# One pool of weight halves for the whole kernel, and one set of four small tiles

## The chip, the core and the metric

The kernel runs on one core of a Trainium2 chip. The metric is the device time of one execution in microseconds (us); the time before is the median of three runs, 2027.32 us. TensorE (PE) multiplies, VectorE (DVE) and ScalarE (ACT) do elementwise work, GpSimd (POOL) does a little elementwise work and issues some DMAs, and SyncE (SP) issues most DMAs.

## What is computed

The reference is a decoder trunk of two layers over one sequence of 256 tokens with width 2048, all in float32. The even layer projects its normed input into two latents (q and kv, 512 wide each), a rotary key of 64 and a pooling input of 1024, runs attention with 8 heads and a pooling mixer, and projects out. The odd layer is a gated short convolution. Each layer ends with a squared-ReLU MLP with hidden width 8192:

```
def _mlp(h, w_up, w_down):
    return jnp.square(jax.nn.relu(h @ w_up)) @ w_down

x = x + jnp.concatenate([a, b], axis=-1) @ even_w_out[e]        # even layer
x = x + _short_conv(h, odd_w_in[o], odd_conv_w[o], odd_w_out[o])  # odd layer
x = x + _mlp(_rmsnorm(x, mlp_norm_g[layer]), w_mlp_up[layer], w_mlp_down[layer])
```

The pooling mixer takes, in four groups of 256 channels, trailing means over 2, 4, 8 and 16 positions minus the token, then a small linear map per group.

## The kernel before

Float32 products are made from two halves: every weight and every activation is split into a part `hi` that the fast float32r format holds and a rest `lo`, and a product is three matmuls (hi by hi, lo by hi, hi by lo).

Weights come in slabs of about 1 MB. `slab` (L123) takes a tile `raw` from a pool of three and issues its DMA on SP (L128). `halved` (L131) then makes for each part of the slab one tile `hi` by a cast on ACT (L140) and one tile `lo` by a subtraction on DVE (L141). The pool `halves` has six buffers of each; a slab takes two of each, so three slabs can be held ready ahead of PE. A `raw` tile is free again when its subtractions are done, a `hi` or `lo` tile when its last matmul is done.

The pools `raws` and `halves` are opened by `new_stage` (L77). It is called with three raw buffers twice: at L213 for the first stage and at L393 after it. The second call closes both pools and opens them anew over the same memory with `reuse_waits="tile"`, which means that a new tile waits for the old tiles that it overlaps. The first stage (`latent_slab`, L334) reads eight slabs of 2 x 1088 columns for the latents and the rotary key, so its `hi` and `lo` rows have 4.25 KB; all later slabs have rows of 4 KB. The tiles of the second opening lie at other addresses than those of the first, and one new tile overlaps two old ones. After L393 the eight slabs of the pooling input follow (loop over the four groups, L463 on), then four slabs of the kv weights and three of the q weights (`widen`, L513), one slab of the pooling map, the output projection with attention woven in, and the MLPs and the convolution. The calls at L714 and L900 keep `raws` and `halves` and only change what lies above them.

Between the last latent matmul and the first pooling matmul stand, on PE, a transpose of gain rows (L238) and, on ACT, six copies out of PSUM (`lat`, L366). The rotary tables are made on DVE from L395 on.

Small tiles come from the pool `small` with two buffers for each name. Name `t` holds the copied half of a PSUM sum (`sum_halves`, L191), the discarded squares (`junk`, L288, L385, L505) and the rotated part (`turned`, L497). Name `u` holds the sum itself, the pooled mean (`pm`, L487) and the sums of forms (`f`, L743). Name `sq` holds the squared hidden values (L731) and the gated values (L943), and `rb` (L315) a spread-out norm factor. All of them have rows of up to 2 KB.

Each engine works through its own queue in order. The order within a queue is not the order of the source: a planner of the framework sets it when the kernel is built, from its own estimate of when each instruction can start, with the source order as priority. `with behind(...)` (L114) adds fixed order at some places. An instruction at the head of a queue that waits for a semaphore stops all behind it. The pooled mean of the last group is split only behind the preparation of the first q slab (L567 to L569).

Of the kernel before, what the change touches and what calls it, by code (L numbers as in the profile page):

```python
# [16 lines left out]
P = 128  # L17
D = 2048
S = 256
# [48 lines left out]
def trunk(ctx: ExitStack, tc, x_in, pos_in, mix_g, mlp_g, w_up, w_down, w_in, pool_in, qa_g, kva_g, w_uq, w_ukv,  # L68
# [8 lines left out]
    def new_stage(raw_bufs=0, **more):  # L77

        for s_ in reversed(stage[1 - bool(raw_bufs):]):
            s_.close()  # L80
        del stage[1 - bool(raw_bufs):]
        for wanted in (dict(raws=raw_bufs, halves=6) if raw_bufs else {}, more):
            if wanted:
                stage.append(ExitStack())
                for name, bufs in wanted.items():
                    pools[name] = stage[-1].enter_context(tc.tile_pool(name=uid(name), bufs=bufs, reuse_waits="tile"))

    pools = {}
    small = ctx.enter_context(tc.tile_pool(name="small", bufs=2))
    acts = ctx.enter_context(tc.tile_pool(name="acts", bufs=4))  # L90
    psum = ctx.enter_context(tc.tile_pool(name="psum", bufs=4, space=PSUM))

# [2 lines left out]
    def uid(s):  # L95
        count[0] += 1
        return f"{s}{count[0]}"
# [4 lines left out]
    def act_tile():  # L102
        return acts.tile([P, 4, 2 * S], F32R, tag="hT", name=uid("hT"))
# [86 lines left out]

    def sum_halves(ps, name):  # L191

        t = small.tile([P, 2, S], F32, tag="t", name=uid("t"))
        nc.scalar.copy(t, ps[:, :, S:2 * S])  # L194
        u = small.tile([P, 2, S], F32, tag="u", name=uid(name))
        nc.vector.tensor_tensor(out=u, in0=ps[:, :, 0:S], in1=t, op=ALU.add)
        return u

    def split(dst_hi, dst_lo, src):
        nc.scalar.copy(dst_hi, src)  # L200
        nc.vector.tensor_tensor(out=dst_lo, in0=src, in1=dst_hi.bitcast(F32), op=ALU.subtract)
# [83 lines left out]
    def squares(ss, b):  # L285

        for t in range(T):
            junk = small.tile([P, NB], F32, tag="t", name=uid("junk"))  # L288
            nc.scalar.activation(junk, x[:, t, b * NB:(b + 1) * NB], AF.Square, accum_out=ss[:, t, b:b + 1])

    def turn_block(xT, b, which, i, then=None):
# [19 lines left out]
    def over_tokens(r, pool):  # L311

        ps = bank2()
        for t in range(T):
            rb = small.tile([P, P], F32, tag="rb", name=uid("rb"))  # L315
            nc.vector.tensor_copy(rb, r[:, t:t + 1].to_broadcast([P, P]))
            nc.tensor.transpose(ps[:, 0, t * P:(t + 1) * P], rb, ident)
        R = pool.tile([P, S], F32, name=uid("R"), bufs=1)
        nc.vector.tensor_copy(R, ps[:, 0, 0:S])
        return R  # L320
# [49 lines left out]
    def latents():  # L370

        lat_ss = ap_.tile([P, 2 * T], F32, name="lat_ss")
        for i, g in ((1, "kva"), (0, "qa")):
            dst = act_tile()
            ps = bank2().rearrange("p a (k s) -> p (a k) s", s=S)
            for k in range(KL):
                c0 = i * LORA + k * P
                for t in range(T):
                    nc.tensor.transpose(ps[:, k, t * P:(t + 1) * P], lat[:, t, c0:c0 + P], ident)
            for k in range(KL):  # L380
                split_scaled(dst[:, k, 0:S], dst[:, k, S:2 * S], ps[:, k, :], gain(g, k))
            latT.append(dst)
        for t in range(T):
            for i in range(2):
                junk = small.tile([P, NB], F32, tag="t", name=uid("junk"))  # L385
                nc.scalar.activation(junk, lat[:, t, i * LORA:(i + 1) * LORA], AF.Square,
                                     accum_out=lat_ss[:, i * T + t:i * T + t + 1])
        rsqrt(lat_r, lat_ss, LORA)
        R0.append(over_tokens(r0, ap_))
# [73 lines left out]
    for g in reversed(range(GROUPS)):  # L463
        ps = bank2()
        for s in range(2):
            ws = slab(pool_in[g, s], 8, 2 * P, sub=4)
            for j in range(8):
                kt = 8 * s + j
                for n in range(2):
                    columns_summed(ps[:, n, 0:S], xT, kt, ws[j], n * P, kt == 0, kt == KD - 1)  # L470
            if s == 0:
                flush()
        if done:
            split_pooled(*done)
        u = ap_.tile([P, 2, PAD + S], F32, tag="s", name=uid("pu"), bufs=4)
        nc.gpsimd.memset(u[:, :, 0:PAD], 0.0)
        nc.vector.tensor_tensor(out=u[:, :, PAD:], in0=ps[:, :, 0:S], in1=twice(R0[0]), op=ALU.mult)
        cur = u
        for st in range(g + 1):
            sh = 1 << st  # L480
            nxt = ap_.tile([P, 2, PAD + S], F32, tag="s", name=uid("pn"), bufs=4)
            if st < g:
                nc.gpsimd.memset(nxt[:, :, 0:PAD], 0.0)
            nc.gpsimd.tensor_tensor(out=nxt[:, :, PAD:], in0=cur[:, :, PAD:], in1=cur[:, :, PAD - sh:PAD + S - sh],  # L484
                                    op=ALU.add)
            cur = nxt
        m = small.tile([P, 2, S], F32, tag="u", name=uid("pm"))  # L487
        nc.gpsimd.tensor_scalar(out=m, in0=cur[:, :, PAD:], scalar1=1.0 / (2 << g), scalar2=None, op0=ALU.mult)
        nc.gpsimd.tensor_tensor(out=m[:, :, 0:PAD], in0=cur[:, :, PAD:2 * PAD],
                                in1=invc[:, g, :].unsqueeze(1).to_broadcast([P, 2, PAD]), op=ALU.mult)  # L490
        nc.gpsimd.tensor_tensor(out=m, in0=m, in1=u[:, :, PAD:], op=ALU.subtract)
        done = g, m

    def rotate(src, t, heads, tables):

        own, other = (a[:, t, :].unsqueeze(1).to_broadcast([P, heads, ROPE]) for a in tables)
        turned = small.tile([P, heads, ROPE], F32, tag="t", name=uid("turned"))  # L497
        for a, b in ((slice(0, HALF), slice(HALF, ROPE)), (slice(HALF, ROPE), slice(0, HALF))):
            nc.vector.tensor_tensor(out=turned[:, :, a], in0=src[:, :, b], in1=other[:, :, a], op=ALU.mult)
        nc.vector.tensor_tensor(out=src, in0=src, in1=own, op=ALU.mult)  # L500
        nc.vector.tensor_tensor(out=src, in0=src, in1=turned, op=ALU.add)

    def square_sum(out_, a):
        n = a.shape[1]
        junk = small.tile([P, NB], F32, tag="t", name=uid("junk"))  # L505
        nc.scalar.activation(junk[:, :n], a, AF.Square, accum_out=out_)


# [201 lines left out]
    def mlp(layer, ss, xT, after=None):  # L710
# [6 lines left out]
        def up_chunk(c):  # L717

            pss = []
            yield from columns_steps(pss, up, xT, c * NB, 4)  # L720
            hT = act_tile()
            seven = c < 2 * (pairs - 1)
            if seven:
                fT = pools["forms"].tile([P, 2, 2, 4, P], F32R, tag="fT", name=uid("fT"))
            hid[c] = hT
            if seven:
                sums[c] = fT
            for i, ps in enumerate(pss):
                u = sum_halves(ps, "h")
                nc.scalar.activation(u, u, AF.Relu)  # L730
                sq = small.tile([P, 2, S], F32, tag="sq", name=uid("sq"))  # L731
                nc.scalar.activation(sq, u, AF.Square)
                split(hT[:, 2 * i:2 * i + 2, 0:S], hT[:, 2 * i:2 * i + 2, S:2 * S], sq)
                if seven:
                    sum_forms(fT[:, i], sq.rearrange("p e (t s) -> p (e t) s", t=T))
                yield
            if not r2:
                r2.append(const.tile([P, T], F32, name=uid("r2")))
                nc.vector.reciprocal(out=r2[0], in_=mean_eps(ss))

        def sum_forms(fT, a):

            f = small.tile([P, 4, P], F32, tag="u", name=uid("f"))  # L743
            nc.vector.tensor_tensor(out=f[:, 0:2, :], in0=a[:, 1:2, :].to_broadcast([P, 2, P]), in1=a[:, 0:4:3, :], op=ALU.subtract)
            nc.vector.tensor_tensor(out=f[:, 2, :], in0=a[:, 3, :], in1=f[:, 0, :], op=ALU.subtract)
            nc.vector.tensor_tensor(out=f[:, 3, :], in0=a[:, 2, :], in1=f[:, 2, :], op=ALU.subtract)
            split(fT[:, 0], fT[:, 1], f)
# [156 lines left out]
    for blk in range(4):  # L904
# [35 lines left out]
        yT.append(yt)  # L940
        for i in range(2):
            u = sum_halves(pss[i], "b")
            y = small.tile([P, 2, S], F32, tag="sq", name=uid("y"))  # L943
            nc.vector.tensor_tensor(out=y, in0=u, in1=accs[i], op=ALU.mult)
            split(yt[:, 2 * i:2 * i + 2, 0:S], yt[:, 2 * i:2 * i + 2, S:2 * S], y)

# [51 lines left out]
```

## Time and profile before

| | us |
|---|---|
| median of the three runs | 2027.32 |
| lowest, highest | 2025.16, 2027.45 |
| the profiled execution, its own time | 2022.49 |
| its span, first to last instruction | 2020.7 |
| PE busy in the span | 2004.3 |
| DVE busy | 1392.5 |
| ACT busy | 1122.9 |
| POOL busy | 101.2 |

Busy times are those of the profiled execution. PE is busy for 99% of the span, so a time is gained or lost only where PE waits or works at a lower clock; the place to look is where the few waits of PE stand and what ends them.

### The profile page before, as it was taken

Reading aid. Unit: us, or ns where it says so; the run is one execution under the profiler, and the core shown is the slowest. Engines: PE = TensorE matmul, PEld = TensorE weight load, DVE = VectorE, ACT = ScalarE, POOL = GpSimd, SP = SyncE. Lnnn points to the kernel's source line nnn. Section 1 sums busy time; section 2 is a strip of 40 time slices with the busy share of each in tenths; the row PEclk is TensorE's granted clock in tenths of the full one; section 3 lists DMA queues with packets and bytes.
Section 4 is the critical chain, followed back from the end, with each engine's and each line's share of the span. In section 5 each row is a group of like instructions: output and inputs, shape, how many; then the busy total and the mean of one; then the engine's idle time right before and its main releaser. Section 6 shows DMA issues by size and latency. Waiting matters only on the chain.

```text
span 2020.7 us, 26714 instructions
## 1 busy us (share of the span) xinstructions
PE 2004.3 (99%) x10534; PEld 1721.2 (85%) x10534; DVE 1392.5 (69%) x1739; ACT 1122.9 (56%) x1480; POOL 101.2 (5%) x132
## 2 busy tenths in 40 slices
PE   8999999999999999999999999999999999999999
PEld 7987888888888888888888888888888888888887
DVE  5767567777767777776566656567776777767774
ACT  5467556655555655555444444456555566555552
POOL 2240000000000000000000000000000000000000
PEclk9999999999999999999999999999999999999999
DMA  7445657887888878765555557658797977879663
GB/s 255 159 168 185 194 202 227 273 250 236 276 260 269 250 237 273 240 211 185 188 188 188 187 188 240 218 188 239 243 278 243 289 231 261 262 249 286 200 219 125
DMA packets 65230, 457.62 MB, mean 226 GB/s; under 512 B 7344, under 2 KB 8240, under 8 KB 10192
## 3 DMA queue, kind: packets, MB, share of 16 engines
q1 hardware_dynamic: 56656, 396.91, 54.7%
q0 software_dynamic: 8416, 59.00, 15.3%
q8 instruction: 82, 1.34, 0.3%
q14 instruction: 44, 0.36, 0.0%
q10 hardware_dynamic: 32, 0.01, 0.0%
HBM read 453.79 MB, written 2.10 MB: 226 GB/s over the span
## 4 chain that ended last, share of the span: by engine, by line
PE 96%; POOL 1%; DMA 1%; DVE 1%; ACT 1%; issue 1%; SPq 0%; ACTq 0%; DVEq 0%; POOLq 0%
PE ps L160 32%; PE ps L161 16%; PE ps L153 10%; PE ps L155 10%; PE ps L154 10%; PE ps L769 4%; PE ps L771 4%; PE ps L770 4%; PE ps L297 1%; DMA raw<-in_even_w_in 1%; POOL pn L484 1%; PE ps L166 1%; PE ps L168 1%; PE ps L167 0%; DVE lo L141 0%
## 5 line engine op out<-in xcount | busy, mean ns | idle before, releaser
L141 DVE TENSOR_TENSOR lo<-raw,hi 128x1024 fp32r<-128x1024 f32 (+2 forms) x694 | 848.0, 1225 | 420.8 <-ACT hi L140 419.2
L140 ACT CAST hi<-raw 128x1024 fp32r<-128x1024 f32 (+2 forms) x694 | 726.1, 1049 | 592.9 <-PE ps L160 340.5
L160 PE MATMUL ps<-xT,hi 128*128 128x512 f32 x2816 | 989.0, 394 | 0.0
L161 PE MATMUL ps<-xT,lo 128*128 128x256 f32 x2816 | 789.5, 280 | 0.0
L160 PEld LDWEIGHTS ps<-xT,hi 128*128 128x128 f32 x2816 | 529.6, 188 | 122.2
L161 PEld LDWEIGHTS ps<-xT,lo 128*128 128x128 f32 x2816 | 527.6, 187 | 3.7
L153 PE MATMUL ps<-hi,hT 128*128 128x512 f32 (+1 forms) x896 | 349.1, 390 | 0.0
L155 PE MATMUL ps<-hi,hT 128*128 128x512 f32 (+1 forms) x896 | 347.3, 388 | 0.0
L154 PE MATMUL ps<-lo,hT 128*128 128x512 f32 (+1 forms) x896 | 347.1, 387 | 0.0
L153 PEld LDWEIGHTS ps<-hi,hT 128*128 128x128 f32 x896 | 168.3, 188 | 35.1 <-issue 1.3
L155 PEld LDWEIGHTS ps<-hi,hT 128*128 128x128 f32 x896 | 168.2, 188 | 34.7
L154 PEld LDWEIGHTS ps<-lo,hT 128*128 128x128 f32 x896 | 168.3, 188 | 33.3
L140 ACT CAST hi<-t 128x1024 fp32r<-128x1024 f32 x84 | 88.1, 1053 | 91.7 <-PE ps L160 50.7
L141 DVE TENSOR_TENSOR lo<-t,hi 128x1024 fp32r<-128x1024 f32 x84 | 102.6, 1221 | 48.7 <-ACT hi L140 48.7
L763 POOL DMA_DIRECT2D t<-in_w_mlp_down x42 | 36.6, 871 | 1135.0 <-DVE lo L141 821.5
L769 PE MATMUL ps<-hi,fT 128*128 128x512 f32 x224 | 88.1, 393 | 0.0
L771 PE MATMUL ps<-hi,fT 128*128 128x512 f32 x224 | 87.7, 391 | 0.0
L770 PE MATMUL ps<-lo,fT 128*128 128x512 f32 x224 | 87.1, 389 | 0.0
L194 ACT COPY t<-ps 128x512 f32<-128x512 f32 x88 | 50.8, 578 | 50.9 <-PE ps L161 50.9
L769 PE MATMUL ps<-hi,hT 128*128 128x512 f32 x168 | 65.8, 392 | 0.0
L771 PE MATMUL ps<-hi,hT 128*128 128x512 f32 x168 | 65.6, 390 | 0.0
L770 PE MATMUL ps<-lo,hT 128*128 128x512 f32 x168 | 65.4, 389 | 0.0
(186 smaller groups left out, 1573.6 us busy)
## 6 DMA issues: line engine op xcount, KB each, us to landing
raw<-in_w_mlp_up SPq DMA_DIRECT2D x128, 1024.0 KB, 5.3
raw<-in_w_mlp_down SPq DMA_DIRECT2D x114, 1024.0 KB, 5.2
raw<-in_odd_w_in SPq DMA_DIRECT2D x48, 1024.0 KB, 4.9
t<-in_w_mlp_down POOLq DMA_DIRECT2D x42, 1024.0 KB, 9.6
raw<-in_even_w_out SPq DMA_DIRECT2D x16, 1024.0 KB, 5.0
raw<-in_odd_w_out SPq DMA_DIRECT2D x16, 1024.0 KB, 5.0
t<-in_w_mlp_down SPq DMA_DIRECT2D x14, 1024.0 KB, 4.8
v<-in_w_mlp_down SPq DMA_DIRECT2D x14, 1024.0 KB, 4.9
```

The costliest lines, as they stand in the source:

```text
L140: a = nc.scalar.copy(h, r)
L141: v = nc.vector.tensor_tensor(out=l, in0=r, in1=h.bitcast(F32), op=ALU.subtract)
L153: nc.tensor.matmul(o, lhsT=a_hi, rhs=hi[:, c0:c0 + n], start=first, stop=False)
L154: nc.tensor.matmul(o, lhsT=a_hi, rhs=lo[:, c0:c0 + n], start=False, stop=False)
L155: nc.tensor.matmul(o, lhsT=a_lo, rhs=hi[:, c0:c0 + n], start=False, stop=last)
L160: nc.tensor.matmul(o, lhsT=hi[:, c0:c0 + P], rhs=act[:, kt, :], start=first, stop=False)
L161: nc.tensor.matmul(o[:, S:2 * S], lhsT=lo[:, c0:c0 + P], rhs=act[:, kt, 0:S], start=False, stop=last)
L194: nc.scalar.copy(t, ps[:, :, S:2 * S])
L763: nc.gpsimd.dma_start(b, at(e, n), accum_op=ALU.add)
L769: nc.tensor.matmul(o, lhsT=a_hi, rhs=hi, start=q == 0, stop=False)
L770: nc.tensor.matmul(o, lhsT=a_hi, rhs=lo, start=False, stop=False)
L771: nc.tensor.matmul(o, lhsT=a_lo, rhs=hi, start=False, stop=q == 3)
```

## The change

The pool of halves is opened once, ahead of all other pools that change, and is no longer part of `new_stage`, which now opens and closes only the raw tiles. Its rows are 4.25 KB throughout. In `small`, the names `t`, `u`, `sq` and `rb` become one name `t` with four buffers of 2 KB; `f` has a name and one buffer of its own. `sum_halves` adds in place, relu squared is squared in place, and the tile of sums of forms is taken inside `sum_forms`.

```diff
-        for wanted in (dict(raws=raw_bufs, halves=6) if raw_bufs else {}, more):
+        for wanted in (dict(raws=raw_bufs) if raw_bufs else {}, more):
...
-    pools = {}
+    pools = dict(halves=ctx.enter_context(tc.tile_pool(name="halves", bufs=6)))
     small = ctx.enter_context(tc.tile_pool(name="small", bufs=2))
+    T4 = dict(tag="t", bufs=4)
...
-        t = small.tile([P, 2, S], F32, tag="t", name=uid("t"))
-        nc.scalar.copy(t, ps[:, :, S:2 * S])
-        u = small.tile([P, 2, S], F32, tag="u", name=uid(name))
-        nc.vector.tensor_tensor(out=u, in0=ps[:, :, 0:S], in1=t, op=ALU.add)
+        u = small.tile([P, 2, S], F32, name=uid(name), **T4)
+        nc.scalar.copy(u, ps[:, :, S:2 * S])
+        nc.vector.tensor_tensor(out=u, in0=ps[:, :, 0:S], in1=u, op=ALU.add)
...
-            junk = small.tile([P, NB], F32, tag="t", name=uid("junk"))
+            junk = small.tile([P, NB], F32, name=uid("junk"), **T4)
...
-            rb = small.tile([P, P], F32, tag="rb", name=uid("rb"))
+            rb = small.tile([P, P], F32, name=uid("rb"), **T4)
...
-        m = small.tile([P, 2, S], F32, tag="u", name=uid("pm"))
+        m = small.tile([P, 2, S], F32, name=uid("pm"), **T4)
...
-        turned = small.tile([P, heads, ROPE], F32, tag="t", name=uid("turned"))
+        turned = small.tile([P, heads, ROPE], F32, name=uid("turned"), **T4)
...
                 nc.scalar.activation(u, u, AF.Relu)
-                sq = small.tile([P, 2, S], F32, tag="sq", name=uid("sq"))
-                nc.scalar.activation(sq, u, AF.Square)
-                split(hT[:, 2 * i:2 * i + 2, 0:S], hT[:, 2 * i:2 * i + 2, S:2 * S], sq)
-                if seven:
-                    sum_forms(fT[:, i], sq.rearrange("p e (t s) -> p (e t) s", t=T))
+                nc.scalar.activation(u, u, AF.Square)
+                split(hT[:, 2 * i:2 * i + 2, 0:S], hT[:, 2 * i:2 * i + 2, S:2 * S], u)
+                sum_forms(c, i, u.rearrange("p e (t s) -> p (e t) s", t=T))
...
-            f = small.tile([P, 4, P], F32, tag="u", name=uid("f"))
+            f = small.tile([P, 4, P], F32, tag="f", name=uid("f"), bufs=1)
...
-            y = small.tile([P, 2, S], F32, tag="sq", name=uid("y"))
+            y = small.tile([P, 2, S], F32, name=uid("y"), **T4)
```

The other discarded squares change their name in the same way. No instruction is added or removed.

## Rows read from the trace of the kernel before

**Rows 1.** The page: busy time by engine, and the chain by engine.
```profile
PE 2004.3 (99%) x10534; PEld 1721.2 (85%) x10534; DVE 1392.5 (69%) x1739; ACT 1122.9 (56%) x1480; POOL 101.2 (5%) x132
...
PE 96%; POOL 1%; DMA 1%; DVE 1%; ACT 1%; issue 1%; SPq 0%; ACTq 0%; DVEq 0%; POOLq 0%
```

**Rows 2.** Stretches: us, busy and count by engine, PE clock, DMA share, GB/s.
```profile
60.00:66.00 6.00, 4.07 (x27) 3.80 (x25) 0.33 (x2) 3.89 (x8) 0.00 (x0) 1.00 0.00 0
67.40:70.80 3.40, 3.40 (x18) 3.40 (x18) 1.96 (x4) 3.40 (x10) 0.47 (x1) 0.50 0.45 106
70.80:74.20 3.40, 3.40 (x31) 3.40 (x30) 3.15 (x4) 3.40 (x6) 0.55 (x1) 1.00 0.50 207
75.00:115.00 40.00, 40.00 (x341) 40.00 (x340) 28.65 (x33) 16.05 (x23) 22.20 (x20) 1.00 0.54 192
115.00:155.00 40.00, 40.00 (x186) 33.42 (x185) 28.32 (x58) 29.85 (x80) 14.36 (x14) 1.00 0.52 187
160.00:2015.00 1855.00, 1855.00 (x9592) 1580.82 (x9591) 1287.69 (x1539) 1029.37 (x1285) 53.31 (x68) 1.00 0.72 229
```

**Rows 3.** Waits of PE: who, for whom, us in total, times, longest.
```profile
PE ps L166 <- ACT hi L140: 1.9, 1, 1.9
PE ps L166 <- ACT qkv L520: 1.9, 1, 1.9
```

**Rows 4.** Timeline of PE: start us, us, instruction [idle before, releaser].
```profile
63.77 0.26 PE L238 MATMUL ps<-ident,rows 112*128 112x112 f32 x1
65.97 0.39 PE L166 MATMUL ps<-xT,hi 128*128 128x256 f32 x1 [1.93 <-ACT hi L140]
```

**Rows 5.** Timeline of ACT, the same moment.
```profile
50.19 0.47 ACT L204 ACTIVATE xT<-ps,gains 128x256 fp32r<-128x256 f32 x1 [0.55 <-DVE xT L205]
62.11 2.87 ACT L366 ACTIVATE lat<-ps,r 128x384 f32<-128x384 f32 x6 [11.45 <-PE ps L155]
64.86 2.00 ACT L140 CAST hi<-raw 128x1024 fp32r<-128x1024 f32 x2
```

**Rows 6.** Timeline of SP's queue: the first DMA issues for the pooling input.
```profile
41.95 0.33 SPq L128 DMA_DIRECT2D raw<-in_pool_in  x1
47.70 0.80 SPq L128 DMA_DIRECT2D raw<-in_pool_in  x2
```

**Rows 7.** DMA issues: count, KB each, median us from issue to landing.
```profile
raw<-in_pool_in SPq DMA_DIRECT2D x8, 1024.0 KB, 4.9
```

**Rows 8.** Timeline of DVE: the spread norm factor, and around the boundary.
```profile
43.08 0.36 DVE L316 COPY rb<-r 128x128 f32<-128x128 f32 x2 [0.85 <-POOL r L362]
...
64.07 0.27 DVE L239 COPY gains<-ps 128x112 f32<-128x112 f32 x1 [5.35 <-PE ps L238]
65.94 2.36 DVE L141 TENSOR_TENSOR lo<-raw,hi 128x1024 fp32r<-128x1024 f32 x2 [1.60 <-ACT hi L140]
```

**Rows 9.** Groups by form to 200 us, ACT: count, busy us, mean ns, idle.
```profile
L140 ACT CAST hi<-raw 128x1024 fp32r<-128x1024 f32 x47 | 47.9, 1048 | 14.5 <-PE ps L155 6.1 <-DMA raw<-in_even_w_out 2.8 <-DMA raw<-in_even_w_uq 2.6
L140 ACT CAST hi<-raw 128x1088 fp32r<-128x1088 f32 x15 | 16.2, 1100 | 7.9 <-DMA raw<-in_even_w_in 5.1 <-PE ps L155 2.7
```

**Rows 10.** Groups over the span: two operations of the MLP on DVE.
```profile
L196 DVE TENSOR_TENSOR h<-ps,t 128x512 f32<-128x512 f32 x64 | 44.0, 687 | 16.7 <-ACT t L194 16.7
...
L744 DVE TENSOR_TENSOR f<-sq 128x256 f32<-128x256 f32 x56 | 23.6, 422 | 8.5 <-ACT sq L732 8.5
```

**Rows 11.** Timeline of ACT: casts ahead of the copies out of PSUM.
```profile
138.06 1.05 ACT L140 CAST hi<-raw 128x1024 fp32r<-128x1024 f32 x1 [2.49 <-DMA raw<-in_even_w_uq]
...
149.31 1.05 ACT L140 CAST hi<-raw 128x1024 fp32r<-128x1024 f32 x1 [2.79 <-DMA raw<-in_even_w_out]
...
155.88 1.25 ACT L520 ACTIVATE qkv<-ps,lat_r 128x512 f32<-128x512 f32 x2
```

**Rows 12.** Timeline of DVE: a rotation, and the last read of a pooled mean.
```profile
88.87 1.42 DVE L499 TENSOR_TENSOR turned<-lat,other 128x32 f32<-128x32 f32 x2
...
138.30 0.69 DVE L201 TENSOR_TENSOR hT<-pm,hT 128x512 fp32r<-128x512 f32 x1
```

More of the change, by code (lines that the diff above doesn't have):

```diff
@@ L384, in latents @@
             for i in range(2):
-                junk = small.tile([P, NB], F32, tag="t", name=uid("junk"))
+                junk = small.tile([P, NB], F32, name=uid("junk"), **T4)
                 nc.scalar.activation(junk, lat[:, t, i * LORA:(i + 1) * LORA], AF.Square,
@@ L504, in square_sum @@
         n = a.shape[1]
-        junk = small.tile([P, NB], F32, tag="t", name=uid("junk"))
+        junk = small.tile([P, NB], F32, name=uid("junk"), **T4)
         nc.scalar.activation(junk[:, :n], a, AF.Square, accum_out=out_)
@@ L720, in up_chunk @@
             yield from columns_steps(pss, up, xT, c * NB, 4)
-            hT = act_tile()
-            seven = c < 2 * (pairs - 1)
-            if seven:
[L724 to L727, printed above, removed]
+            hT = hid[c] = act_tile()
             for i, ps in enumerate(pss):
@@ L730, in up_chunk @@
                 nc.scalar.activation(u, u, AF.Relu)
-                sq = small.tile([P, 2, S], F32, tag="sq", name=uid("sq"))
-                nc.scalar.activation(sq, u, AF.Square)
-                split(hT[:, 2 * i:2 * i + 2, 0:S], hT[:, 2 * i:2 * i + 2, S:2 * S], sq)
-                if seven:
-                    sum_forms(fT[:, i], sq.rearrange("p e (t s) -> p (e t) s", t=T))
+                nc.scalar.activation(u, u, AF.Square)
+                split(hT[:, 2 * i:2 * i + 2, 0:S], hT[:, 2 * i:2 * i + 2, S:2 * S], u)
+                sum_forms(c, i, u.rearrange("p e (t s) -> p (e t) s", t=T))
                 yield
@@ L739, in up_chunk, with sum_forms @@
                 nc.vector.reciprocal(out=r2[0], in_=mean_eps(ss))
-        def sum_forms(fT, a):
-            f = small.tile([P, 4, P], F32, tag="u", name=uid("f"))
+        def sum_forms(c, i, a):
+            if c >= 2 * (pairs - 1):
+                return
+            if i == 0:
+                sums[c] = pools["forms"].tile([P, 2, 2, 4, P], F32R, tag="fT", name=uid("fT"))
+            fT = sums[c][:, i]
+            f = small.tile([P, 4, P], F32, tag="f", name=uid("f"), bufs=1)
             nc.vector.tensor_tensor(out=f[:, 0:2, :], in0=a[:, 1:2, :].to_broadcast([P, 2, P]), in1=a[:, 0:4:3, :], op=ALU.subtract)
```

## The prediction

> **What bounds the kernel now.** First the page: PE is busy 2004.3 us of 2020.7, 99%, and 96% of the chain that ended last is PE's own matmuls [rows 1]. So the busy times of DVE and ACT do not matter as such; only a moment in which PE stands still, or works at the lower clock, can be won or lost. Next the table by stretches: from 160 us to the end PE is busy 1855.00 of 1855.00 us at clock 1.00 [rows 2]. There run both MLPs, with all 64 squared-ReLU sums and all 56 sums of forms that the diff rewrites [rows 10], and no wait there reaches PE. From 75 to 155 us PE is busy throughout too. What is left is the first 160 us, and there the waits of PE name two places after the start: one wait of 1.9 us for ACT's cast `hi`, and one of 1.9 us for ACT's copy `qkv` out of PSUM [rows 3].
>
> The first stands at the stage boundary of L393, which the diff touches. PE ends the latent matmuls and transposes the gain rows at 63.77; the first pooling matmul comes at 65.97, after 1.93 us of waiting [rows 4]. ACT's timeline shows why: it ran nothing from 50.7 us on, then waited 11.45 us at the head of its queue for PE, made the six copies `lat` from 62.11, and only then, at 64.86, the first two casts of a pooling slab [rows 5]. The slab itself was long there: its DMA was issued at 41.95, the next two at 47.70 [rows 6], and such a DMA lands 4.9 us after its issue [rows 7], so the first was in by about 46.9. DVE had sat idle 5.35 us before 64.07 and began the subtractions at 65.94 [rows 8]. Data and both engines were free, hence what kept the casts behind 62.11 was either room for `hi` and `lo` or the planned order. In the code the room is the plain candidate: the second pool lies over the first at other addresses, and its first tiles overlap tiles that the last two latent slabs still fill.
>
> [...]
>
> **Part by part.**
>
> *One pool of halves.* With a ring that goes on, the first pooling halves take the buffers of the sixth latent slab, two before the last. A latent slab is 36 matmuls; at the pace of the stretch from 60 to 66 us (27 in 4.07 us busy [rows 2]) that is 5.4 us, so these buffers are free two slabs before 63.8, near 53 us, and the next pair near 58. ACT, idle until 62.11, can then make the casts of two slabs (4 x 1.05 = 4.2 us, the mean from [rows 9]) before the latents end, and DVE the first subtractions (2.36 for two [rows 8]) in its idle 5.35 us. PE then goes from the transpose at 63.77 + 0.26 = 64.03 straight to pooling; it also needs PSUM, and the first of the three `lat` banks is emptied by about 63.1 (two of six copies, 2.87 us in all [rows 5]). Term: -1.93 us, bounds -1.93 (no standstill) and 0 (the order stays). I take -1.93, since raw, ACT and DVE are all free for longer than the casts take.
>
> *The clock.* If PE does not stand still, the half-clock stretch should go: -1.4 us, bounds -1.4 and 0. I take -1.4, as no other standstill stands before it.
> [...]
>
> *Does it travel to the end?* After 64 us the pooling chain on POOL, DVE and ACT starts from PE's finished groups, so it moves ahead with PE. What was late next stays next: the 1.9 us for `qkv` near 157 us [rows 3]. Its cause is further on: casts that stand in ACT's queue ahead of the PSUM copies and wait for DMAs (2.49 us at 138.06, 2.79 us at 149.31), so that a copy comes only at 155.88 [rows 11]. I take it as moved, not changed: 0, bounds -1.9 and +8.4 (three such waits of 2.79 more).
>
> *Rows of 4.25 KB.* The first stage already uses this pitch: a cast of 1088 columns takes 1100 ns, one of 1024 takes 1048 [rows 9], 1.01 and 1.02 ns a column. Cost 0; the bounds, one hundredth of ACT's casts either way, lie under PE's work.
>
> *In place.* The copy of half a sum, the addition, relu, square and the split are the same operations on the same engines in the same order. The wait of DVE for ACT's copy, 16.7 us over 64 times [rows 10], stays, since the addition still reads what the copy wrote. Nothing is queued behind it that PE waits for after 160 us. 0, bounds 0 and 0.5 us for each of the 16 chunks if the tile came free later; PE's full stretch [rows 2] hides that.
>
> *`f` with one buffer.* The next `f` is written on DVE after the last subtraction of the one before, which stands ahead of it in the same queue; that one has waited for ACT already. Two `f` of a chunk lie a slab apart. 0.
>
> *Four tiles for all.* `rb` is written at 43.08 [rows 8], long before its transposes, and holds two of the four until then; the last pooled mean holds one until its split ends at 138.30 + 0.69 [rows 12]. So two or three are left for squares and rotations, where there were two. The squares are written by ACT alone, in order, and wait for nobody. 0; below, a gain is excluded since nothing waited for these tiles. Above: if tiles were handed out strictly in turn, the second rotation of the rotary key would wait for that last mean and its work, three pieces at most like the 1.42 us at 88.87 [rows 12], some 4.3 us by estimate, would fall into DVE's busy stretch from 115 us on (28.32 of 40.00 [rows 2]); it has the cover of idle DVE there.
>
> **Sum.** -1.93 - 1.4 = -3.3 us. The profiled execution took 2022.49 us and would take 2019.2; it lies 4.8 us under the median of the runs, 2027.32, more than they spread (2.3 us), so the change is carried over: 2027.3 - 3.3 = 2024.0 us.
>
> **Rivals.**
> *The order stays (0.18).* The planner may have put the casts behind the `lat` copies for a reason of its own, say that it expects the slab later than it lands. For it: the trace shows an order, not a wait for room. Against it: the slab was in 15 us before. Then nothing changes: 2027.3 us.
> *The second wait goes too (0.15).* With two slabs made ahead, ACT has 4.2 us less to do after 64 us, and the copies may come before the casts that wait. For it: ACT is busy 29.85 of 40.00 us from 115 to 155 [rows 2], so it isn't full. Against it: those waits are for DMAs, which three raw tiles limit as before. -3.3 - 1.9 = -5.2: 2022.1 us.
> *Slower: more casts stand ahead of the copies (0.12).* A planner that sees room for halves earlier puts casts earlier into ACT's queue, where they wait for DMAs in front of the `qkv` copies; PE runs out of PSUM. Place: the seven slabs of kv and q weights, 115 to 157 us. Price: up to 2.79 us for each [rows 11]; from two more on the gain is gone, with three it is 8.4 - 3.3 = +5.1: 2032.4 us. Against it: room for halves is limited there by PE's pace in both versions.
>
> **How the numbers follow.** The forecast, -3.3 with the order otherwise kept, gets 0.55; its own range is 2021 to 2026. The range over the cases starts at 2020.0, below the case with both waits gone by the spread of the runs, and ends at 2029.5, which takes in the unchanged time with the same spread and part of the slower case. A measurement of this kernel can tell 0.2%, 4.05 us, from no change, and the forecast lies just inside it. Faster by more: two fifths of the forecast's chance plus nearly all of the both-waits case, 0.36. Slower by more: most of the slower case and a little for the unknown bounds, 0.11. Within: 0.53.
>
> **What would show it.** Right: ACT's first casts of a pooling slab begin before 60 us, ahead of the `lat` copies; PE's row for L166 waiting on `hi` is gone; no stretch at clock 0.50 after 60 us; the same steps after 160 us about 3.3 us earlier. Wrong: casts still behind the `lat` copies; or PE's waits near 155 us grow; or PE below full in any stretch after 160 us, which would speak for the small tiles.

## The result, and the profile after

The changed kernel takes 2036.14 us (median of 5 runs, 2035.41 to 2037.12), the kernel before 2025.78 beside it on the same chip: ratio 1.0050, 95% interval 1.0035 to 1.0064. It is 10.4 us slower; 2024.0 with a range from 2020.0 to 2029.5 was forecast.

The page after, busy time by engine and the chain, as [rows 1]: DVE, ACT and POOL are busy as long as before within 4 us, TensorE (PE) 16.3 us longer with the same 10,534 matmuls.
```profile
PE 2020.6 (99%) x10534; PEld 1724.8 (85%) x10534; DVE 1396.1 (69%) x1739; ACT 1120.6 (55%) x1480; POOL 100.5 (5%) x132
...
PE 98%; DMA 1%; ACT 1%; DVE 0%; SPq 0%; issue 0%
```

What was forecast at the boundary came. PE's timeline, as [rows 4]: the pooling matmul follows the transpose of the gain rows at once.
```profile
67.87 0.26 PE L238 MATMUL ps<-ident,rows 112*128 112x112 f32 x1
67.90 0.36 PE L167 MATMUL ps<-xT,hi 128*128 128x256 f32 x1
```
ACT's timeline, as [rows 5]: five casts of pooling slabs now stand ahead of the six `lat` copies, the first at 54.63.
```profile
54.63 1.04 ACT L141 CAST hi<-raw 128x1024 fp32r<-128x1024 f32 x1
56.20 1.05 ACT L141 CAST hi<-raw 128x1024 fp32r<-128x1024 f32 x1 [0.53 <-PE ps L156]
...
65.13 1.05 ACT L141 CAST hi<-raw 128x1024 fp32r<-128x1024 f32 x1 [1.92 <-PE ps L156]
66.21 2.87 ACT L366 ACTIVATE lat<-ps,r 128x384 f32<-128x384 f32 x6
```
PE's waits, as [rows 3]: both rows of 1.9 us are gone. One of 1.0 us (ending at 160.65) stands where the second was. Of the two rows from the first 30 us, the one for `xT` was 1.2 us and the one for `hi` 2.6.
```profile
PE ps L154 <- ACT xT L204: 3.7, 1, 3.7
PE ps L154 <- ACT hi L141: 2.5, 1, 2.5
PE ps L605 <- DVE hT L205: 1.0, 1, 1.0
```
The same two rows in the kernel before:
```profile
PE ps L153 <- ACT hi L140: 2.6, 1, 2.6
...
PE ps L153 <- ACT xT L204: 1.2, 1, 1.2
```
The stretches, as [rows 2] (the boundary is 4.1 us later here, so the windows are too): 44 matmuls where there were 27, and clock 1.00 in the two behind it, where one was at 0.50. But from 160 us on PE is again as good as full, at clock 1.00, and starts 9,504 matmuls where it started 9,592.
```profile
64.00:70.00 6.00, 6.00 (x44) 5.99 (x43) 4.53 (x21) 4.84 (x10) 0.00 (x0) 1.00 0.60 205
71.40:74.80 3.40, 3.40 (x31) 3.40 (x31) 2.48 (x3) 3.00 (x5) 1.01 (x1) 1.00 0.11 12
74.80:78.20 3.40, 3.40 (x31) 3.40 (x30) 3.21 (x8) 2.36 (x7) 0.00 (x0) 1.00 0.89 337
75.00:115.00 40.00, 40.00 (x336) 40.00 (x335) 23.19 (x26) 15.29 (x21) 22.45 (x22) 1.00 0.50 179
...
160.00:2015.00 1855.00, 1854.35 (x9504) 1569.43 (x9505) 1288.04 (x1527) 1023.97 (x1278) 52.59 (x67) 1.00 0.72 229
```
That is the loss: the same instructions, hardly a wait, full clock, slower pace. It is read from the starts. A matmul's `lhsT` has a load of its own ahead of it in the profile (PEld at L160, 128x128: from 1099.69 for the matmul at 1099.81, 188 ns in the mean) and is called stationary here; its `rhs`, 512 or 256 columns in PE's rows, is called streamed. The up-projections of the MLPs and the input projection of the convolution use one helper (`columns_out`); both are called up-projections here. They come in pairs: `xT` streamed against the stationary `hi` (512 columns), then against `lo` (256 columns). From 1,000 to 1,220 us, in the convolution, both kernels run nothing else on PE. PE's row of that window (us, busy and count, clock, DMA share, GB/s), before:
```profile
1000.00:1220.00 220.00, 220.00 (x1263) 1.00 0.55 188
```
and after:
```profile
1000.00:1220.00 220.00, 220.00 (x1247) 1.00 0.54 187
```
So a pair takes 2 x 220/1263 = 348.4 ns before and 352.8 after. In the timeline, before:
```profile
1099.81 0.39 PE L160 MATMUL ps<-xT,hi 128*128 128x512 f32 x1
1100.04 0.28 PE L161 MATMUL ps<-xT,lo 128*128 128x256 f32 x1
1100.16 0.39 PE L160 MATMUL ps<-xT,hi 128*128 128x512 f32 x1
...
1100.86 0.39 PE L160 MATMUL ps<-xT,hi 128*128 128x512 f32 x1
```
three pairs in 1.05 us; after, 1.06, with some steps from `hi` to `lo` of 0.24 instead of 0.23:
```profile
1100.17 0.40 PE L161 MATMUL ps<-xT,hi 128*128 128x512 f32 x1
1100.40 0.28 PE L162 MATMUL ps<-xT,lo 128*128 128x256 f32 x1
1100.52 0.40 PE L161 MATMUL ps<-xT,hi 128*128 128x512 f32 x1
1100.76 0.28 PE L162 MATMUL ps<-xT,lo 128*128 128x256 f32 x1
...
1101.23 0.40 PE L161 MATMUL ps<-xT,hi 128*128 128x512 f32 x1
```
The durations beside the starts overlap (0.39 from 1099.81 on, with the next start 0.23 later); the starts are what to read.

The output projections and the down-projections stream the halves against a stationary `hT`; all are called down-projections here. A block of 120 of them (the convolution's output projection) stands alone behind that stretch, first and last row before:
```profile
1237.62 0.40 PE L153 MATMUL ps<-hi,hT 128*128 128x512 f32 x1
...
1264.60 0.39 PE L155 MATMUL ps<-hi,hT 128*128 128x512 f32 x1
```
and after:
```profile
1246.45 0.39 PE L154 MATMUL ps<-hi,hT 128*128 128x512 f32 x1
...
1273.69 0.39 PE L156 MATMUL ps<-hi,hT 128*128 128x512 f32 x1
```
26.98/119 = 226.7 ns each before, 228.9 after.

A ledger of both profiles: how much later the matmul of the same number starts after than before (PE's order is the same but for 50 of 10,534).

| matmul (its time before, us) | after minus before |
|---|---|
| 300 (60.4) | +4.1 |
| 450 (82.6) | +0.6 |
| 900 (153.9) | +1.5 |
| 1200 (211.2) | 0.0 |
| 4800 (914.8) | +5.4 |
| 8800 (1675.4) | +11.8 |
| last (2017.0) | +14.6 |

The boundary gave 3.5 us, the pooling stage took back 0.9, the second standstill gave 1.5; from there 14.6 us are lost evenly. Added up from start to start behind matmul 1,200, the 2,816 pairs take 8.4 us more (their mean after 160 us goes from 349.6 to 352.5 ns), the 2,375 down-projections there 4.9, and the 1,176 matmuls of the combinations (helper `product` in the MLP) 1.3. Without the 4.1 us of the start the ledger ends at 10.5, the medians at 10.4.

### The profile page after: what moved, and what is told of

Its sections match the earlier page's. It is cut to its first block, busy times and chain, and to the rows that moved or that the text cites. A ratio compares the mean times of both kernels' runs of the same rounds, so it can differ in the third digit from the quotient of the medians.

```text
span 2035.3 us, 26740 instructions
## 1 busy us (share of the span) xinstructions
PE 2020.6 (99%) x10534; PEld 1724.8 (85%) x10534; DVE 1396.1 (69%) x1739; ACT 1120.6 (55%) x1480; POOL 100.5 (5%) x132
## 4 chain that ended last, share of the span: by engine, by line
PE 98%; DMA 1%; ACT 1%; DVE 0%; SPq 0%; issue 0%
PE ps L161 32%; PE ps L162 16%; PE ps L154 11%; PE ps L156 11%; PE ps L155 11%; PE ps L768 4%; PE ps L766 4%; PE ps L767 4%; PE ps L167 1%; PE ps L168 1%; PE ps L169 1%; DMA raw<-in_even_w_in 1%; PE ps L297 1%; PE ps L613 0%; PE ps L617 0%; ACT junk L506 0%
## 5 line engine op out<-in xcount | busy, mean ns | idle before, releaser
L857 DVE SCALAR_TENSOR_TENSOR x<-ps,r,x 128x512 f32<-128x512 f32 (+1 forms) x73 | 50.9, 737 | 14.8 <-PE ps L156 14.8
```

What stands on the lines that cost most here:

```text
L857: nc.vector.scalar_tensor_tensor(out=xb, in0=ps[:, t, :n], scalar=r2[0][:, t:t + 1], in1=xb, op0=ALU.mult, op1=ALU.add)
```

## The experiments

What the change did to the layout is in the compiled programs: the halves went from 138,464 bytes into a partition to 67,360, while `xT` stayed at 34,592, and `hT` went from 81,120 to 130,272. In the table D is the start of the halves less that of `xT`, E that of `hT` less that of the halves, both modulo 256; all slots of a kernel have the same D and E. "Pair" is the mean start to start of up-projection pairs after 160 us, "x" the number of matmuls from 1,000 to 1,220 us, "down" the mean start to start of the 120 block, in ns. The names of 5 to 7 and the expectations give places modulo 128, and the 225.5 ns of the expectations is a mean over all down-projections, not the block of the table. The ratio is to the kernel before, beside it on the chip.

| kernel | D | pair | x | E | down | median us | ratio (95%) |
|---|---|---|---|---|---|---|---|
| before | 192 | 349.6 | 1263 | 0 | 226.7 | 2025.8 to 2027.7 | 1 |
| changed | 0 | 352.5 | 1247 | 192 | 228.9 | 2036.14 | 1.0050 (1.0035 to 1.0064) |
| 1 changed, halves +64 | 64 | 353.3 | 1248 | 0 | 226.9 | 2030.96 | 1.0024 (1.0015 to 1.0034) |
| 2 before, halves +64 | 0 | 351.2 | 1247 | 192 | 229.0 | 2040.22 | 1.0069 (1.0057 to 1.0082) |
| 3 changed, halves +32 | 32 | 353.0 | 1248 | 32 | 233.3 | 2051.57 | 1.0125 (1.0111 to 1.0139) |
| 4 changed, halves +96 | 96 | 347.4 | 1271 | 224 | 233.3 | 2035.80 | 1.0047 (1.0033 to 1.0061) |
| 5 xT 32, h 0, hT 0 | 96 | 347.2 | 1271 | 0 | 227.1 | 2012.80 | 0.9938 (0.9921 to 0.9955) |
| 6 xT 0, h 96, hT 96 | 96 | 347.2 | 1271 | 0 | 227.1 | 2012.91 | 0.9937 (0.9921 to 0.9954) |
| 7 all 0 | 0 | 350.7 | 1271 | 0 | 227.0 | 2023.65 | 0.9994 (0.9982 to 1.0006) |
| 8 as 1, lo 512 further | 64 | 353.3 | 1247 | 0 | 226.9 | 2029.89 | 1.0013 (1.0002 to 1.0023) |
| 9 before, one gap of 32 | 224 | 347.4 | 1272 | 0 | 226.8 | 2019.71 | 0.9969 (0.9956 to 0.9981) |
| 10 small tiles alone | 192 | 350.8 | 1248 | 0 | 226.8 | 2029.66 | 1.0010 (1.0001 to 1.0019) |
| 11 small tiles and pitch | 192 | 350.8 | 1248 | 0 | 226.9 | 2029.41 | 1.0010 (1.0001 to 1.0019) |
| 12 before once more | 192 | 349.6 | 1263 | 0 | 226.7 | 2027.96 | 1.0007 (0.9996 to 1.0017) |
| 13 shared pool behind acts | 192 | 350.8 | 1247 | 0 | 226.8 | 2023.17 | 0.9989 (0.9980 to 0.9998) |
| 14 as 13, one gap of 32 | 224 | 347.4 | 1271 | 0 | 226.8 | 2011.62 | 0.9934 (0.9921 to 0.9946) |
| 15 before, one gap of 128 | 64 | 353.3 | 1249 | 0 | 226.9 | 2035.81 | 1.0055 (1.0041 to 1.0069) |

A gap is a small tile in a pool of its own. These are the two of run 1, 64 bytes each; 3 has 32 and 96 bytes, 4 has 96 and 32:
```diff
+gap = ctx.enter_context(tc.tile_pool(name="gap", bufs=1)).tile([P, 16], F32, name="gap")
+nc.gpsimd.memset(gap, 0.0)
 pools = dict(halves=ctx.enter_context(tc.tile_pool(name="halves", bufs=6)))
+gap2 = ctx.enter_context(tc.tile_pool(name="gap2", bufs=1)).tile([P, 16], F32, name="gap2")
+nc.gpsimd.memset(gap2, 0.0)
```

**Runs 1 to 4: place or layout.** 2 has the gaps of 1 in the kernel before, around each stage's halves in `new_stage`.

1: 

> The changed kernel with a gap of 64 bytes a partition ahead of the pool of weight halves and another behind it. The halves begin 64 bytes further on; pitch, order, small tiles and sharing stay. In the kernel before, every half of the up-projections began at a multiple of 128 bytes plus 96; in the changed kernel at a multiple plus 32. Theory A (where a half begins within 128 bytes sets TensorE's pace): the fp32r pair of an up-projection goes back from about 353 to 349 ns, over 2816 pairs about 10 us, so about 2026 us, and with the boundary gains that stay about 2022 to 2026. Theory B (the region the halves lie in, or the pitch of 4.25 KB between them): 2036 as the changed kernel. Theory C (small tiles, relu squared in place): 2036.

2: 

> The kernel before with a gap of 64 bytes a partition ahead of each stage's pool of halves and another behind it; halves of each stage then begin at a multiple of 128 bytes plus 32, as in the changed kernel, with nothing else of the change. Theory A: the up-projection pair goes from 349 to about 353 ns, 10 to 13 us slower, about 2036 to 2039 us, spread over the whole run. Theory B and C: 2026 us, as before.

3: 

> The changed kernel with 32 bytes ahead of the halves and 96 behind: halves begin at a multiple of 128 bytes plus 64. Theory A in the form that only the place within 64 bytes matters is already excluded by the traces of before and after (both plus 32 there), so theory A gives a third value here: between 2022 and 2040. Theories B and C: 2036 us.

4: 

> The changed kernel with 96 bytes ahead of the halves and 32 behind: halves begin at a multiple of 128 bytes. [...] Theories B and C: 2036 us.

Run 2 is plain: 64 bytes in the kernel before, with nothing of the change, cost 13 us. Run 1 gave back about half: the down-projections were at once as before (226.9), the up-projections were not (353.3, where 349 was expected). Run 3 shows how far it goes, 25 us. Theory A stood, but not as a matter of the halves' own place: in 4 the up-projections were at their best and the down-projections at their worst.

**Runs 5 to 8: each operand, or the two together.** 5: gaps of 96 and 64; 6 and 7: also 96 bytes ahead of `big`, and 96 and 64, or 0 and 64, around the halves; 8: `lo` in a pool of its own with 512 bytes ahead.

5: 

> The changed kernel with gaps of 96 bytes ahead of the halves and 64 behind. Start within 128 bytes: xT 32, halves 0, the operand tiles hT 0 (in the run with 96 ahead and 32 behind: 32, 0, 96). Theory A1 (what counts is how far apart the two operands of a matmul begin, modulo 128: the down-projections, halves against hT, were quickest at a difference of 0, 225.5 ns, and 3 to 6 ns slower at 64 and 32): up-projections stay at 347.4 ns a pair, down-projections fall from 231.4 to 225.5 ns, 2,688 of them 16 us, so about 2020 us. Theory A2 (what counts is where the streamed operand begins by itself): halves at 0 stay as slow as in that run, 2036 us.

6: 

> The changed kernel with all from x on 96 bytes further: xT 0, halves 96, hT 96 within 128 bytes. Theory A1 (difference of the two operands): up-projections as at xT 32 and halves 0 (the same difference), 347.4 ns a pair, and down-projections 225.5 ns: about 2020 us. Theory A2 (each operand by itself): down-projections 225.5 ns as halves at 96 had, up-projections unknown, since xT moves to another place: 2015 to 2040.

7: 

> The changed kernel with xT, halves and hT all at a multiple of 128 bytes. Theory A1: up-projections as in the changed kernel (difference 0, about 352.5 ns a pair), down-projections 225.5 ns: about 2028 us. [...]

8: 

> The changed kernel with 64 bytes more ahead of the halves, and the lo slots moved a further 512 bytes away from the hi slots, so that hi and lo of one block lie 26,624 bytes apart (a multiple of 2,048, as 24,576 in the kernel before; 26,112 in the changed kernel). All else as in the run with 64 bytes ahead (353.3 ns a pair, 2031 us). Theory D (the distance of hi from lo, which the pitch of 4.25 KB changes, sets the up-projections' pace): back to 349.6 ns, about 2020.5 us. Theory E (the pitch between slots or the region): 353.3 ns, 2031 us.

For the down-projections, halves at 0 are slow against `hT` at 96 (233.3) and quick against `hT` at 0 (227.1): it is the distance of the two operands. 5 and 6 have other places and the same distances, and agree in every column. Both came 7 us below the 2020 expected, since the combinations gained as well: 7.3 us from 4 to 5, added up from start to start. First and last row of the block of 120 in run 4, 27.76 us,
```profile
1241.92 0.39 PE L158 MATMUL ps<-hi,hT 128*128 128x512 f32 x1
...
1269.68 0.39 PE L160 MATMUL ps<-hi,hT 128*128 128x512 f32 x1
```
and in run 5, 27.02:
```profile
1230.60 0.40 PE L158 MATMUL ps<-hi,hT 128*128 128x512 f32 x1
...
1257.62 0.39 PE L160 MATMUL ps<-hi,hT 128*128 128x512 f32 x1
```
All operands at multiples of 128 bytes (7) is not the best place (2023.65 us against 2012.80 in 5). Run 7 also runs at 346.7 ns from 1,020 to 1,200 us, where the changed kernel, with the same D of 0, runs at 353.3; so for the pairs D alone does not settle the pace. The distance of `hi` from `lo`, changed by 512 bytes in 8, made no difference to it (353.3 as in 1).

**Runs 9 to 12: the parts of the change, and the start.** 9: 32 bytes ahead of `acts` in the kernel before. 10: the changed kernel with `pools = {}` and `dict(raws=raw_bufs, halves=6)` again. 11: as 10 and
```diff
-hi = pools["halves"].tile([P, sub, cols], F32R, tag="hi", name=uid("hi"))
+hi = pools["halves"].tile([P, 1088], F32R, tag="hi", name=uid("hi"))[:, :sub * cols].rearrange("p (s c) -> p s c", s=sub)
```
and `lo` alike.

9: 

> The kernel before with one gap of 32 bytes a partition ahead of the pool of operand tiles (acts), nothing else: hT and halves then begin at multiples of 128 bytes, xT stays at a multiple plus 32, the places of the fastest run so far. Theory A1 (the difference of the two operands' starts within 128 bytes): up-projections 349.6 to 347.3 ns a pair (6.5 us), down-projections unchanged at 225.5 ns, the combinations a little quicker, so 2018 to 2021 us against 2027; and the change itself, at these places (2012.8), is worth the 5 to 6 us of the two boundary waits. Rival theory F (the placement explains all of it and the sharing of the pool gives nothing): 2013 us. Rival theory G (placement helps the shared pool alone): 2027 us.

10: 

> The kernel before with the small tiles, relu squared in place and f of its own as in the changed kernel, but with halves opened by each stage; operand tiles and halves begin 3 KB earlier and stay at a multiple of 128 bytes plus 96, as before. Theory A1 (placement): the waits of before stay, TensorE's pace stays at 349.6 ns a pair: 2027 us. The rival that small tiles or the chain in place cost time: 2030 us or more, with waits on u or f in the rows of VectorE and ScalarE that hold TensorE.

11: 

> As the run with the small tiles alone, and every half in rows of 4.25 KB in all stages, still opened by each stage, starts at a multiple of 128 bytes plus 96. Theory E1 (the pitch of 4,352 bytes between slots slows the up-projections at this place): 353.3 ns a pair, about 10 us slower, 2037 us. Theory E2 (it is the region of the SBUF in which the shared pool lies): 349.6 ns, 2027 us.

12: 

> The kernel before, unchanged, for a second profile of its first stage. If the 4.1 us that the changed kernel lost before 30 us come from run to run in the landing of the first slabs, this profile shows the second slab's cast later than 15.6 us and a half-clock stretch after 20 us, about as the changed kernel; if they come from the change, the cast stands at 15.6 us again and the span at 2020.7.

9 came as forecast: with the place alone the kernel before gains 7.9 us, and the shared pool at such a place about 7 more (14.9 us in 5 and 14.5 in 14, each against the kernel before beside it). 10 and 11 agree, so the pitch of 4.25 KB costs nothing, and the small tiles cost no wait: from matmul 1,300 to 4,800 their lag behind the first profile of before stays the same within 0.1 us. Both lose 3.1 us in one stretch, from 960 to 1,260 us, where pairs take 353.3 ns, and run at 349.0 in the MLPs on either side. PE's row of that window in run 10:
```profile
1000.00:1220.00 220.00, 220.00 (x1248) 1.00 0.55 187
```
12 answers for the start. ACT's second slab cast and PE's window from 20 to 30 us, first profile of before:
```profile
15.61 2.10 ACT L140 CAST hi<-raw 128x1088 fp32r<-128x1088 f32 x2 [4.15 <-DMA raw<-in_even_w_in]
```
```profile
20.00:30.00 10.00, 9.70 (x62) 9.73 (x63) 7.62 (x10) 8.42 (x14) 0.00 (x0) 1.00 0.86 315
```
the same kernel once more:
```profile
16.45 2.10 ACT L140 CAST hi<-raw 128x1088 fp32r<-128x1088 f32 x2 [4.91 <-DMA raw<-in_even_w_in]
```
```profile
20.00:30.00 10.00, 9.15 (x49) 8.90 (x48) 7.74 (x11) 8.08 (x14) 0.00 (x0) 0.83 0.86 313
```
and the changed kernel:
```profile
17.91 2.10 ACT L141 CAST hi<-raw 128x1088 fp32r<-128x1088 f32 x2 [6.94 <-DMA raw<-in_even_w_in]
```
```profile
20.00:30.00 10.00, 9.37 (x42) 8.88 (x43) 8.33 (x11) 7.47 (x14) 0.00 (x0) 0.68 0.91 347
```
In the second profile of before the cast is 0.8 us late and the clock falls as well; matmul 75 stood 2.4 us later than in the first, 4.1 in the changed kernel. The other runs settle the rest: in the five more profiles that open the halves by stage (2, 9, 10, 11, 15) matmul 75 stands 2.8 to 5.1 us later than in the first profile, in the ten with the shared pool from 0.9 earlier to 4.9 later. So the loss at the start goes with the landing of the first slabs from execution to execution, and no run shows a part of it that belongs to the change. The first profile of before was a lucky one, as its place under the median said, and at the second wait too: in 9, 10, 11, 12 and 15 a stretch of 3.4 us at clock 0.50 follows that wait of 1.9 to 2.3 us (in 12 from 161.5 to 164.9), in the first profile none does.

**Runs 13 to 15: region, or the low bits.** 13: the `halves` line moved behind `acts`; 14: also 32 bytes ahead of `acts`; 15: 128 bytes ahead of `acts` in the kernel before.

13: 

> The changed kernel with the shared pool opened behind the operand tiles (acts) instead of ahead of the small tiles; starts within 128 bytes are then those of before by themselves: xT 32, halves 96, hT 96. Down-projections 225.5 ns by theory A1. Theory E2 (the region): up-projections go back to 349.0 ns a pair, about 2020 us. Theory H (the pace is one of two at this distance, and how a stretch is entered decides, not the region): 353.3 in some stretches or all, 2021 to 2032 us.

14: 

> As the run behind the operand tiles, with one gap of 32 bytes ahead of acts, so that halves and hT begin at multiples of 128 bytes and xT at a multiple plus 32. Theory A1: 347 ns a pair in every stretch whatever the region, 225.4 ns for the down-projections, 2012 to 2015 us as the best run so far; a version with one line moved and one gap that beats the kernel before by 0.6%. Theory E2: the region could move it, 2012 to 2022 us.

15: 

> The kernel before with a gap of 128 bytes ahead of the operand tiles: all starts within 128 bytes stay (xT 32, halves and hT 96). Theory A1 with places of 128 bytes alone: 349.6 ns a pair and 2027 us, as before. Theory H or a dependence on more than the low 7 bits: some stretch at 353.3, up to 2037 us.

15 keeps every place within 128 bytes, and its up-projections go from 349.0 to 353.3 ns in every stretch, as in 1 and 8, which also have D 64; the five profiles at D 192 have 349.0 in both MLPs. So 128 is too small a period, and 256 fits these runs; no run moves an operand by 256 alone. That also fits run 1, whose D is 64 and not 192. 13, at D 192, is back at 349.0 in both MLPs, in a quite other region, so there the region is out. It has the 353.3 stretch of 10 and 11, which before has not, at the same D and E; what makes that stretch slow stays open. 14 is the version to keep, the change with one line moved and one gap: 0.66% faster than the kernel before and 1.2% faster than the change as it was. PE's row there:
```profile
1000.00:1220.00 220.00, 220.00 (x1271) 1.00 0.55 189
```

## Why the prediction was wrong

- *What bounds the kernel.* The step that failed is the sentence that "only a moment in which PE stands still, or works at the lower clock, can be won or lost", which the part on the time before says as well. A third thing can: the pace at which a full PE at full clock starts its matmuls. The rows showed 1855.00 of 1855.00 us busy [rows 2], and busy time does not show pace: after, it is 1854.35 with 88 starts fewer. The change moved every half by 71,104 bytes, which took D from 192 to 0 and E from 0 to 192, and no term of the sum asked what that does to PE. In the two profiles it was worth +14.6 us; runs 2 and 15 make 13 and about 10 us from a gap alone.
- *Rows of 4.25 KB, cost 0.* Right in its number (run 11), but it looked at ACT's casts only; the new pitch was the visible half of the new layout, the start address the half that cost.
- *One pool of halves, -1.93, and the clock, -1.4.* Right in size, and in how the wait goes: -3.3 forecast, 3.5 measured (3.5 to 4.0 in all ten profiles with the shared pool), with the casts ahead of the copies, the wait for `hi` gone and no stretch at 0.50. But no run shows the 1.4 us as the price of the standstill; it is an estimate from the 18 and 31 matmuls of [rows 2], and in runs 2 and 10 the same wait of 1.94 us stands at the boundary and no such stretch follows. What the runs showed in its place is the 3.5 us for both terms together, and 1.3 us where run 12 has such a stretch behind the second wait and the first profile of before has none.
- *Does it travel to the end?* It did, and the second wait, taken as moved but not changed, mostly went: ACT's last `qkv` copies begin at 154.76 instead of 155.88 [rows 11], with one cast between them and the pair of copies before instead of two; PE waits 1.0 us where it waited 1.9. Beside run 12, whose second wait has its half-clock stretch, this is worth more: from matmul 900 to 1,200 run 12 loses 1.3 us on the first profile and the changed kernel gains 1.5. That rival (0.15) had this part right; its 2022.1 us missed the pace.
- *In place, `f`, four tiles, 0 each.* Run 10 shows no wait from them. The last sign named against the forecast, PE below full after 160 us, is there (0.65 us) but is the rest of the second wait, not the small tiles.
- *The slower rival* (more casts ahead of the `qkv` copies, 2032.4 us) came nearest to the time for a reason that did not occur: fewer casts stand there, and PE waits less.
- *Carrying the change to the median.* At the distances of before (run 13) the sharing gives 2023.17 us, near the 2024.0 forecast and 3.0 under the kernel before beside it. That is in part luck: the gain at the second wait, which the sum put at 0, is offset by the 3.1 us of the stretch at 353.3 ns. Most of the 4.8 us between profile and median were the start and the missing half-clock stretch: run 12's profiled execution is 3.7 us longer, 2.4 and 1.3 of it there.

## What to carry to other kernels

A change that re-sizes or moves pools can move the operands of TensorE (here the halves by 71,104 bytes); compare matmul starts, not busy time, and work out the distance of the streamed from the stationary operand before and after, modulo the 256 that fits these runs. Where the starts differ, one gap of 32 bytes is a cheap experiment; it can win 8 us (run 9) or, with another one behind the halves, cost 15 more (run 3). Judge a layout change only at equal distances, or the 0.3% that sharing gives is hidden under 0.7% of pace.

## What the runs showed of the hardware

For the 512-column fp32r matmuls that stream halves against `hT`, E alone ordered all seventeen profiles (sixteen layouts): 0 took 226.7 to 227.1 ns, 192 took 228.9 to 229.0, 32 and 224 took 233.3. For the up-projection pairs D of 96 or 224 took 347.2 to 347.4 ns in every run, 64 353.3, 32 353.0. At D 192 and 0 the pace differed by stretch (349.0 or 353.3 at 192; in run 7, at 0, 346.7 from 1,020 to 1,200 us and about 352.8 in the MLPs). What decides there, and why two operations like different distances, stays open; all pools of these kernels begin at multiples of 32 bytes, so a finer step was not tried.

So with E the same matmul went from 226.7 to 233.3 ns. The recorded weight loads against `hT` are as long before (E 0, 187.8 ns in the mean of 2,688) as after (E 192, 187.9), and the cause stays open.

Two more readings are from the kernel before. Four float32 matmuls of 256 columns (L613, at 166.70) take 1.06 us from start to start, 265 ns each, where a float32r matmul of 512 columns takes 226.7. And ACT stood idle for 2.79 us until 149.31 at a cast that waited for a DMA [rows 11]; only behind it, from 150.26, came the two `qkv` copies of a sum whose last matmul had started at 147.28.
